# MLP up products of a two-model chain as seven quarter products

## The chip, the cores and the metric

The kernel runs on one core of a Trainium2 chip. The metric is the device time of one execution in microseconds (us). The engines are named as in the profile: PE is TensorE (PEld its weight loads), DVE is VectorE, ACT is ScalarE, POOL is GpSimd, SP is SyncE, which issues the weight transfers.

## What is computed

A first model of two layers (convolution and retention) is followed by a second of two layers: a state-space mixer with an MLP, and an attention over latents (MLA) with an MLP. All weights and activations are float32, 512 tokens of 1024 features; the second model puts 16 meta tokens ahead, so its first layer has 528. What matters here is the second model's frame and its MLPs:

```python
def rms_norm_2(x, gain):
    xf = x.astype(jnp.float32)
    y = xf * lax.rsqrt(jnp.mean(xf * xf, axis=-1, keepdims=True) + EPS)
    return (y * gain.astype(jnp.float32)).astype(x.dtype)

def sqrelu_mlp(h, w_up, w_down):            # w_up 1024 x 4096, w_down 4096 x 1024
    return jnp.square(jax.nn.relu(h @ w_up)) @ w_down

    for i in range(DEPTH):                  # DEPTH = 2
        hn = rms_norm_2(h, ln_mix[i])
        h = h + (ssd_mixer if i % 2 == 0 else mla_mixer)(hn, ...)
        h = h + sqrelu_mlp(rms_norm_2(h, ln_mlp[i]), mlp_w_up[i], mlp_w_down[i])
    return h[:, N_META:]
```

## The kernel before

Activations lie in SBUF with features on the 128 partitions and tokens along the free axis; the residual `xres` has 8 such feature tiles (k = 0 to 7) of 528 tokens. Products keep float32 accuracy by splitting each operand into a high and a low part (type fp32r): the high part is a cast on ACT, the low part a subtraction on DVE. A product is three matmuls, high x high, high x low and low x high, summed in PSUM: `mm3` (L226) with the weights stationary and the tokens moving, `mm3t` (L233) the other way round. PSUM has eight banks: `pb0` and `pb1` hold two each, `side0` to `side3` one each (`BANK[0]` to `BANK[7]`).

Weights come through `Stream`: a plan of tiles in the order of use, two buffers deep. `next(key)` hands out one tile and emits the next one: its transfers on SP's queue into `wraw`, four casts of 512 columns on ACT (L65, `whi`) and four low parts on DVE (L66, `wlo`). An order of instructions per engine is settled by a scheduler from the program's order and dependencies; each engine then runs its own list strictly in order.

The places that are touched:

- *State-space output passes* (`out_pass`, L746). The mixer's 16 result tiles `mix` (split pairs in a ring of nine buffers, `mixh`/`mixl`) are multiplied by the output weights in three passes of 8, 6 and 2 tiles. The last pass adds the last 2 tiles to all 8 feature tiles k and, tile by tile, adds into `xres` (L756, DVE), prepares the operand of the MLP (`prep`: gain and high part on ACT L218, low part on DVE L219) and sums the squares (`sq_acc`: squares on ACT L263, running sum on POOL L264). Then `rstd2` turns the sums into 1/rms: one matmul with ones (L269), a square root on ACT, a reciprocal on DVE (L274).
- *First MLP* (528 tokens as two halves of 264). Four blocks f; in each, four up steps (q; one weight tile of 1024 x 256) and four down steps (1024 x 256 each). An up step makes two feature tiles of 128 hidden columns: `dense2` with 8 feature tiles x 3 matmuls x 2 halves each; relu on ACT (L948), then on DVE a multiplication by R2, the square of 1/rms (L950), one by the relu (L951), and the split into the ring (L254 ACT, L255 DVE). The eight results of a block are then multiplied by the down tiles and added into `xres` (L963).
- *MLA setup* (`mla_setup`) stands in the second block of the first MLP.
- *MLA output passes and second MLP* (512 tokens). Two output passes of four result tiles each, the second with `prep` and `sq_acc`; then the same four blocks: up steps with 512 columns per matmul, down steps with tokens stationary (`mm3t`, 256 columns) into `rt`, token-major, added on DVE (L1310); the transposes of `xres` into `rt` stand after the first block's up steps.

## Time and profile before

| | us |
|---|---|
| runs | 2557.51, 2559.8, 2561.83 (median 2559.8) |
| profiled execution, its own time | 2556.87 |
| its span | 2555.1 |
| PE busy in it | 2500.3 |
| DVE busy | 1480.3 |
| ACT busy | 1001.2 |
| POOL busy | 182.6 |

The span is the time from the first to the last instruction in the profile; the execution's own time has 1.8 us around it. A row of the timeline has the start and the recorded length of one instruction or of several in a row (x2); recorded lengths of neighbours on one engine can overlap, so a cadence is read from starts. The view of waits counts idle time of an engine, put down to the instruction whose end released it. "Granted clock" (PEclk) is TensorE's clock as a share of its higher level.

### The profile page before, as it was taken

The page shows a single profiled execution, that of the slowest core. Times are in us where ns is not written, and L with a number is a line of the kernel's source. Part 1 is how long each engine was busy: PE and PEld are TensorE (multiplying, and loading weights), DVE is VectorE, ACT ScalarE, POOL GpSimd, SP SyncE. Part 2 cuts the span into 40 slices and gives each one's busy share as a digit, 9 for nine tenths or more (in the row PEclk, how much of TensorE's full clock was granted, in tenths as well). Part 3 has the DMA queues.
Part 4 walks back from the last instruction along what each step waited for, and adds up shares of the span by engine and source line. Part 5 has one row for each costly group of instructions (what it writes and reads, how often), then busy time and mean ns, then how long its engine had stood idle before and what let it go on. Part 6 is the DMA issues. An engine that isn't in the chain of part 4 may idle for free.

```text
span 2555.1 us, 40242 instructions
## 1 busy us (share of the span) xinstructions
PE 2500.3 (98%) x16657; PEld 2209.6 (86%) x16657; DVE 1480.3 (58%) x2893; ACT 1001.2 (39%) x2164; POOL 182.6 (7%) x208
## 2 busy tenths in 40 slices
PE   8989999999999999999999999999999999999999
PEld 7878888888888888899999999999997667799898
DVE  6733455474435555888848875434455765644443
ACT  4322333343223334555535543322344764423322
POOL 1000000010000001122112220000011000100000
PEclk9999999999999999999999999999999999999999
DMA  4443222223332222333333322323222111232322
GB/s 142 91 99 108 83 67 83 83 71 94 99 107 66 83 86 61 89 101 96 99 91 93 88 90 87 99 83 99 84 69 72 60 54 50 83 92 90 99 93 73
DMA packets 213383, 220.88 MB, mean 86 GB/s; under 512 B 8796, under 2 KB 203469, under 8 KB 213200
## 3 DMA queue, kind: packets, MB, share of 16 engines
q1 hardware_dynamic: 208512, 207.50, 26.6%
q0 software_dynamic: 4208, 10.68, 2.4%
q8 instruction: 130, 2.13, 0.3%
q14 instruction: 53, 0.43, 0.1%
q10 hardware_dynamic: 480, 0.13, 0.0%
HBM read 215.46 MB, written 2.83 MB: 85 GB/s over the span
## 4 chain that ended last, share of the span: by engine, by line
PE 86%; DVE 5%; ACT 3%; issue 3%; DMA 2%; POOL 1%; POOLq 0%; ACTq 0%; DVEq 0%
PE pb L226 53%; PE main L226 10%; PE main L233 8%; PE pb L233 4%; PE side L1221 1%; PE side L1234 1%; DMA ea<-ssd_a_log 1%; DVE wlo L66 1%; PE side L822 1%; PE main L1227 1%; PE side L831 1%; POOL sums L264 1%; PE side L560 1%; PE side L578 1%; PE side L580 1%
## 5 line engine op out<-in xcount | busy, mean ns | idle before, releaser
L65 ACT CAST whi<-wraw 128x512 fp32r<-128x512 f32 (+2 forms) x721 | 408.4, 622 | 886.2 <-PE pb L226 558.3
L66 DVE TENSOR_TENSOR wlo<-wraw,whi 128x512 fp32r<-128x512 f32 (+2 forms) x721 | 483.1, 711 | 209.6 <-ACT whi L65 208.5
L226 PE MATMUL pb<-xh_n,wlo 128*128 128x264 f32 (+3 forms) x1264 | 352.9, 325 | 0.0
L226 PE MATMUL pb<-xh_n,whi 128*128 128x264 f32 (+3 forms) x1264 | 348.5, 324 | 2.8 <-ACT xh_n L218 2.2
L226 PE MATMUL pb<-xl_n,whi 128*128 128x264 f32 (+3 forms) x1264 | 348.0, 324 | 0.0
L226 PEld LDWEIGHTS pb<-xh_n,whi 128*128 128x128 f32 (+1 forms) x1264 | 213.4, 188 | 23.0 <-ACT xh_n L218 2.5
L226 PEld LDWEIGHTS pb<-xh_n,wlo 128*128 128x128 f32 (+1 forms) x1264 | 214.6, 188 | 19.4 <-issue 1.4
L226 PEld LDWEIGHTS pb<-xl_n,whi 128*128 128x128 f32 (+1 forms) x1264 | 213.4, 188 | 17.7
L226 PE MATMUL pb<-xh_l,whi 128*128 128x512 f32 (+1 forms) x480 | 184.3, 384 | 12.1 <-ACT whi L65 11.0
L226 PE MATMUL pb<-xl_l,whi 128*128 128x512 f32 (+1 forms) x480 | 184.6, 385 | 0.8 <-DVE xl_l L219 0.8
L226 PE MATMUL pb<-xh_l,wlo 128*128 128x512 f32 (+1 forms) x480 | 184.0, 383 | 0.0
L233 PE MATMUL main<-whi,mh_w 128*128 128x256 f32 x512 | 144.3, 282 | 0.1
L233 PE MATMUL main<-whi,ml_w 128*128 128x256 f32 x512 | 143.5, 281 | 0.0
L233 PE MATMUL main<-wlo,mh_w 128*128 128x256 f32 x512 | 143.5, 281 | 0.0
L226 PEld LDWEIGHTS pb<-xh_l,whi 128*128 128x128 f32 x480 | 91.1, 190 | 31.3 <-ACT whi L65 11.8
L226 PEld LDWEIGHTS pb<-xl_l,whi 128*128 128x128 f32 x480 | 91.3, 190 | 18.4 <-DVE xl_l L219 1.2
L226 PEld LDWEIGHTS pb<-xh_l,wlo 128*128 128x128 f32 x480 | 91.2, 190 | 17.6 <-DVE wlo L66 0.2
L226 PE MATMUL pb<-xh_m,whi 128*128 128x264 f32 x512 | 104.5, 285 | 0.1
L226 PE MATMUL pb<-xl_m,whi 128*128 128x264 f32 x512 | 104.5, 285 | 0.0
L226 PE MATMUL pb<-xh_m,wlo 128*128 128x264 f32 x512 | 104.4, 285 | 0.0
L226 PE MATMUL pb<-ml_u,whi 128*128 128x264 f32 x512 | 104.0, 284 | 0.0
L226 PE MATMUL pb<-mh_u,whi 128*128 128x264 f32 x512 | 103.7, 284 | 0.0
(545 smaller groups left out, 5557.8 us busy)
## 6 DMA issues: line engine op xcount, KB each, us to landing
wraw<-w_in SPq DMA_DIRECT2D x64, 1024.0 KB, 6.0
wraw<-mlp_w_up SPq DMA_DIRECT2D x32, 1024.0 KB, 5.6
wraw<-mlp_w_down SPq DMA_DIRECT2D x32, 1024.0 KB, 5.1
wraw<-w_out SPq DMA_DIRECT2D x16, 1024.0 KB, 5.1
wraw<-ssd_w_in SPq DMA_DIRECT2D x16, 1024.0 KB, 5.3
wraw<-ssd_w_in SPq DMA_DIRECT2D x16, 512.0 KB
ab<-acsD POOLq DMA_DIRECT2D x32, 256.0 KB, 3.8
wraw<-ssd_w_out SPq DMA_DIRECT2D x5, 1024.0 KB
```

Source lines behind the costliest of these rows:

```text
L65: nc.scalar.copy(hv[s], rv[s])
L66: eng.tensor_tensor(lv[s], rv[s], hv[s].bitcast(F32), ALU.subtract)
L226: nc.tensor.matmul(ps, w[wq][:, k, wsl], x(xq, k, cs), start=(k == 0 and wq + xq == 0), stop=(k == nk - 1 and wq == 1))
L233: nc.tensor.matmul(ps, x(xq, k, ts_), w[wq][:, k, csl], start=(k == 0 and wq + xq == 0), stop=(k == nk - 1 and xq == 1))
L264: nc.gpsimd.tensor_tensor(dst, dst, v, ALU.add)
L560: nc.tensor.matmul(ch(A, c), ch(kT, c), ch(qT, c), start=True, stop=True)
L578: nc.tensor.matmul(ch(op, c), ch(pm, c), v[:, c, P * n : P * n + P], start=True, stop=(c == 0))
L580: nc.tensor.matmul(ch(op, c), ch(qT, c), ch(st, c - 1), start=False, stop=True)
L822: nc.tensor.matmul(o, xd[:W, h], M[:W, h, :W], start=True, stop=(c == 0))
L831: nc.tensor.matmul(st[:, :256], Bt[:W], xw[:W].rearrange("p h e -> p (h e)"), start=True, stop=True)
L1221: nc.tensor.matmul(sp_, Qh[:, h, q0 : q0 + M], Kh[:, h, :L], start=True, stop=False)
L1227: nc.tensor.transpose(pst[:, c, :M], p[:M, P * c : P * c + P], ident[:M, :M])
```

## The change

*Quarter products.* The 1024 x 256 weight tile is seen as a 2 x 2 of quarters (inner dimension in two halves of 512, hidden columns in two halves of 128), the operand as a 2 x 2 (inner halves, token halves). Seven products of quarters and sums of quarters give the four result quarters, with products numbered 1 to 7 (`m`): weights 11, 12, S4, 22, S1, S2, S3 against operands 11, 21, 22, T4, T1, T2, T3. Each is 4 inner tiles x 3 matmuls of half the tokens, into the next of the eight PSUM banks (`ringpos`). Product 1 is copied to SBUF by ACT (`su`), which empties its bank; seven DVE additions make the results. `Stream.seven` makes the weight sums: S1 to S3 in a scratch `wsr` with one buffer, S4 in place of the quarter 21 of the raw tile, each split by itself (`wsh`, `wsl`, three buffers each), and one cast and one low part over all 2048 columns. `Seven.prep` makes the operand sums T1 to T4, by pairs of feature tiles (k, k + 4), with scratch from the ring of nine. Relu and square are both on ACT now, and R2 is applied after the down products: in the first MLP by a second DVE instruction, in the second by one that takes R2 as a column per token.

*Output passes.* The state-space passes are now: 8 result tiles to all k; 6 to k = 0, 4, 1, 5 (weight tiles j = 0, 1 of two column stretches each); the last 2 to the same four; all 8 to k = 2, 6, 3, 7. Of these the last two, with `prep` by pairs, stand in the first MLP's scope. The second MLA pass goes by the same pairs.

*Later squares.* `sq_acc` moves from the output passes into the first two up steps, four tiles in each, and `rstd2` (in the second MLP `rstd` and four transposes for the column form of R2) behind the third.

The diff, cut to its core:

```diff
+    def seven(self, i, raw, hi, lo):
+        sr = self.spool.tile([P, 3, 512], F32, tag="wsr", name=f"wsr{i}", bufs=1)
...
+        def sums(n):
+            h, l = (self.spool.tile([P, 512], F32R, tag=f"ws{q}", name=f"ws{q}{i}{n}", bufs=3) for q in "hl")
+            nc.scalar.copy(h, sr[:, n])
+            V.tensor_tensor(l, sr[:, n], h.bitcast(F32), ALU.subtract)
+            return [t.rearrange("p (k c) -> p k c", k=4) for t in (h, l)]
...
+        V.tensor_tensor(s1, w["S4"], w["22"], ALU.add)
+        V.tensor_tensor(s3, w["11"], w["S4"], ALU.subtract)
+        V.tensor_tensor(s2, s1, w["11"], ALU.subtract)
+        V.tensor_tensor(w["S4"], w["12"], s2, ALU.subtract)
+        S1, S3 = sums(0), sums(1)
+        nc.scalar.copy(hi, raw)
+        V.tensor_tensor(lo, raw, hi.bitcast(F32), ALU.subtract)
+        S2 = sums(2)
...
+        def prep(self, k, g):
...
+            g_ = scratch("mixh", f"xg{j}")
+            nc.scalar.activation(g_, xres[:, k + 4 * j, hl], AF.Identity, scale=g)
+            a0, a1 = g_[:, :hw], g_[:, hw:]
+            if j == 0:
+                t = scratch("mixl", "xs")
+                V.tensor_tensor(t[:, :hw], a1, a0, ALU.subtract)
+                part(H[:, h0], L[:, h0], a0)
+                part(H[:, h1], L[:, h1], t[:, :hw])
+                self.raw[k] = g_, t
+                return
+            b, t = self.raw[k]
+            t2, t3, t4 = t[:, :hw], t[:, hw:], b[:, :hw]
+            V.tensor_tensor(t3, a1, b[:, hw:], ALU.subtract)
+            part(H[:, hl], L[:, hl], g_)
+            V.tensor_tensor(t2, a1, t2, ALU.subtract)
+            V.tensor_tensor(t4, a0, t2, ALU.subtract)
...
+    def product7(w, X, tmp, nm, order):
...
+        for n in order:
+            a, b = m[n]
+            ps = BANK[ringpos[0]][:, : X.hw]
+            ringpos[0] = (ringpos[0] + 1) % 8
+            for k in range(4):
+                for wq, xq in ((0, 0), (0, 1), (1, 0)):
+                    nc.tensor.matmul(ps, w[wq][a][:, k], X(xq, b, k), start=(k == 0 and wq + xq == 0),
+                                     stop=(k == 3 and wq == 1))
+            B[n] = ps
+            if n == 1:
+                B[1] = tmp("U", f"s{nm}", 4)
+                nc.scalar.copy(B[1], ps)
...
+    def up7(w, X, pool, cs, nm, first=False, bufs=3):
...
+        for n, i, p1, p2 in product7(w, X, tmp, nm, (1, 5, 2, 3, 7, 6, 4) if first else (5, 7, 6, 1, 3, 4, 2)):
+            o = r[n][:, X.hw * i : X.hw * i + X.hw]
+            V.tensor_tensor(o, p1, p2, ALU.add)
+        for n in range(2):
+            nc.scalar.activation(r[n], r[n], AF.Relu)
+            nc.scalar.activation(r[n], r[n], AF.Square)
+            m = mix_tile(f"{nm}{n}")
+            split(m, r[n], cs)
...
-                for n in range(2):
-                    nm = f"{f}{q}{n}"
-                    ps = dense2(w, n, X, 8)
-                    r = tmp(f"r{nm}")
-                    nc.scalar.activation(halves(r), ps, AF.Relu)
-                    t = mp.tile([P, T2], F32, tag="t", name=f"t{nm}", bufs=3)
-                    V.tensor_tensor(t, r, R2, ALU.mult)
-                    V.tensor_tensor(t, t, r, ALU.mult)
-                    m = mix_tile(f"u{nm}")
-                    split(m, t, slice(0, T2))
-                    mix.append(m)
+                mix += up7(w, X, mp, slice(0, T2), f"u{f}{q}", f + q == 0)
+                if f == 0 and q < 2:
+                    for k in range(4 * q, 4 * q + 4):
+                        sq_acc(tmp, sums, k, xres[:, k], f"ssq{k}")
+                if f == 0 and q == 2:
+                    rstd2(Rx, sums, D, BANK[4:6])
+                    V.tensor_tensor(R2, Rx, Rx, ALU.mult)
...
-                    xk = halves(xres[:, k])
-                    V.tensor_tensor(xk, ps, xk, ALU.add)
+                    t = tmp(f"d{f}{k}")
+                    V.tensor_tensor(halves(t), ps, halves(R2), ALU.mult)
+                    V.tensor_tensor(xres[:, k], t, xres[:, k], ALU.add)
...
-                    V.tensor_tensor(rt[:, b, ds_], ps, rt[:, b, ds_], ALU.add)
+                    V.scalar_tensor_tensor(rt[:, b, ds_], ps, R2[:, b : b + 1], rt[:, b, ds_], ALU.mult, ALU.add)
```

How it moves instructions is shown at three places. In the names the number after `wsh`, `whi` or `wraw` is the weight tile's (for `wsh` and `wsl` a last digit 0, 1, 2 stands for S1, S3, S2); the number behind the last underscore tells buffers apart.

PE, between two products of an up step in the first MLP. Before, where one tile of 128 hidden columns ends and the next begins (each row is two matmuls, one per half of the tokens):

```order
L226 MATMUL pb0_77<-xh1_m0_13269,whi131_15362 128x264 x2
L226 MATMUL pb0_77<-xl1_m0_13271,whi131_15362 128x264 x2
L226 MATMUL pb0_77<-xh1_m0_13269,wlo131_15363 128x264 x2
L226 MATMUL pb1_78<-xh0_m0_13268,whi132_15488 128x264 x2
L226 MATMUL pb1_78<-xl0_m0_13270,whi132_15488 128x264 x2
L226 MATMUL pb1_78<-xh0_m0_13268,wlo132_15489 128x264 x2
```

Now, in the second up step of the first block (tile 115), where product 1 ends and product 5, that of S1, begins:

```order
L326 MATMUL side2_72<-xh0_m0_13119,wlo115_13500 128x264
L326 MATMUL side2_72<-xh0_m0_13119,whi115_13499 128x264
L326 MATMUL side2_72<-xl0_m0_13121,whi115_13499 128x264
L326 MATMUL pb1_78<-xh0_m0_13119,wsh1150_13508 128x264
L326 MATMUL pb1_78<-xl0_m0_13121,wsh1150_13508 128x264
L326 MATMUL pb1_78<-xh0_m0_13119,wsl1150_13509 128x264
```

A bank now takes 12 matmuls of one half instead of 48 of both. In this step 12 matmuls of S3, 12 of S2 and 11 of product 1 stand ahead of those of S1, which in the program's order are not ahead of it.

DVE, in a later block of the first MLP, the third of four up steps. Before (`wraw`, `whi`, `wlo`: weight tile; `t`, `r`: result before the split):

```order
L950 TENSOR_TENSOR t210_15550<-r210_15548,R2_13446 128x528
L951 TENSOR_TENSOR t210_15550<-t210_15550,r210_15548 128x528
L255 TENSOR_TENSOR ml_u210_15554<-t210_15550,mh_u210_15553 128x528
L66 TENSOR_TENSOR wlo133_15615<-wraw133_15616,whi133_15614 128x512
L950 TENSOR_TENSOR t211_15607<-r211_15605,R2_13446 128x528
L66 TENSOR_TENSOR wlo133_15615<-wraw133_15616,whi133_15614 128x512
L951 TENSOR_TENSOR t211_15607<-t211_15607,r211_15605 128x528
L66 TENSOR_TENSOR wlo133_15615<-wraw133_15616,whi133_15614 128x512 x2
L255 TENSOR_TENSOR ml_u211_15611<-t211_15607,mh_u211_15610 128x528
L950 TENSOR_TENSOR t220_15676<-r220_15674,R2_13446 128x528
L951 TENSOR_TENSOR t220_15676<-t220_15676,r220_15674 128x528
L255 TENSOR_TENSOR ml_u220_15680<-t220_15676,mh_u220_15679 128x528
```

Now (`uu`, `vu`: partial sums; `ru`: results; L90 to L93 the weight sums):

```order
L90 TENSOR_TENSOR wsr132_15657<-wraw132_15655 128x512
L337 TENSOR_TENSOR uu20_15596<-side2_72,su20_15594 128x264
L91 TENSOR_TENSOR wsr132_15657<-wraw132_15655 128x512
L340 TENSOR_TENSOR vu20_15598<-uu20_15596,side0_70 128x264
L92 TENSOR_TENSOR wsr132_15657<-wsr132_15657,wraw132_15655 128x512
L359 TENSOR_TENSOR ru201_15545<-side1_71,vu20_15598 128x264
L346 TENSOR_TENSOR uu20_15596<-uu20_15596,side1_71 128x264
L359 TENSOR_TENSOR ru200_15544<-pb0_77,vu20_15598 128x264
L359 TENSOR_TENSOR ru200_15544<-pb1_78,su20_15594 128x264
L93 TENSOR_TENSOR wraw132_15655<-wraw132_15655,wsr132_15657 128x4x128
L359 TENSOR_TENSOR ru201_15545<-pb0_77,uu20_15596 128x264
L96 TENSOR_TENSOR wlo132_15654<-wraw132_15655,whi132_15653 128x2048
```

The seven additions of the step's products stand among the sums and low parts for the next weight tile, whose 2048-wide low part (L96) comes ahead of the split of the step's first result.

ACT, in the first block of the first MLP. Before, the second step's results beside the casts of the next weight tiles:

```order
L254 CAST mh_u001_13571<-t001_13568 128x528
L948 ACTIVATE r010_13635<-pb1_78 128x528
L254 CAST mh_u010_13640<-t010_13637 128x528
L65 CAST whi117_13701<-wraw117_13703 128x512
L948 ACTIVATE r011_13692<-pb0_77 128x528
L65 CAST whi117_13701<-wraw117_13703 128x512 x3
```

Now, from just behind the cast of S1 of the third tile (`wsh1160`) and the first relu of the first step (`ru000`):

```order
L411 ACTIVATE ssq1_13632<-xres_93 128x528
L363 ACTIVATE ru000_13522<-ru000_13522 128x528
L84 CAST wsh1161_13654<-wsr116_13645 128x512
L402 CAST mh_u000_13621<-ru000_13522 128x528
L362 ACTIVATE ru001_13523<-ru001_13523 128x528
L411 ACTIVATE ssq2_13635<-xres_93 128x528
L363 ACTIVATE ru001_13523<-ru001_13523 128x528
L411 ACTIVATE ssq3_13638<-xres_93 128x528
L402 CAST mh_u001_13627<-ru001_13523 128x528
L95 CAST whi116_13641<-wraw116_13643 128x2048
L84 CAST wsh1162_13660<-wsr116_13645 128x512
L332 COPY su01_13714<-side2_72 128x264
```

The squares for the norm (L411), relu and square of the first step's results (L362, L363) and the casts for the third tile stand ahead of `su01`, the copy of the second step's product 1.

## Rows read from the trace of the kernel before

**Rows 1.** The profile's page, span and busy time per engine.
```profile
span 2555.1 us, 40242 instructions
PE 2500.3 (98%) x16657; PEld 2209.6 (86%) x16657; DVE 1480.3 (58%) x2893; ACT 1001.2 (39%) x2164; POOL 182.6 (7%) x208
```

**Rows 2.** Waits of PE: line, waited for, us in total, times, longest.
```profile
PE side L269 <- POOL sums L264: 5.0, 4, 2.5
PE side L269 <- POOL asums L264: 1.2, 1, 1.2
PE pb L226 <- DVE xres L756: 0.9, 1, 0.9
```

**Rows 3.** First MLP by stretch: length, PE, PEld, DVE, ACT, POOL, PEclk, DMA share, GB/s.
```profile
1526.00:1574.00 48.00, 48.00 (x394) 48.00 (x394) 30.66 (x47) 18.27 (x32) 0.00 (x0) 1.00 0.33 102
```

**Rows 4.** Timeline of PE in the MLPs: start us, us, line, operation, tiles, shape.
```profile
1540.01 0.41 PE L226 MATMUL pb<-xh_m,wlo 128*128 128x264 f32 x2
...
1556.16 0.41 PE L226 MATMUL pb<-xh_m,wlo 128*128 128x264 f32 x2
...
2211.67 0.39 PE L226 MATMUL main<-xh_m,whi 128*128 128x512 f32 x1
...
2224.88 0.39 PE L226 MATMUL main<-xh_m,whi 128*128 128x512 f32 x1
...
2249.80 0.28 PE L233 MATMUL main<-whi,mh_w 128*128 128x256 f32 x1
...
2257.96 0.29 PE L233 MATMUL main<-whi,mh_w 128*128 128x256 f32 x1
```

**Rows 5.** Timeline of DVE in an up step; in brackets idle time and releaser.
```profile
1546.05 0.69 DVE L66 TENSOR_TENSOR wlo<-wraw,whi 128x512 fp32r<-128x512 f32 x1 [2.82 <-ACT whi L65]
1546.66 0.70 DVE L950 TENSOR_TENSOR t<-r,R 128x528 f32<-128x528 f32 x1
1547.28 0.68 DVE L66 TENSOR_TENSOR wlo<-wraw,whi 128x512 fp32r<-128x512 f32 x1
...
1552.18 0.71 DVE L950 TENSOR_TENSOR t<-r,R 128x528 f32<-128x528 f32 x1 [1.77 <-ACT r L948]
1552.92 0.71 DVE L951 TENSOR_TENSOR t<-t,r 128x528 f32<-128x528 f32 x1
```

**Rows 6.** Groups by line: busy us, mean ns of one, idle before, releasers.
```profile
L1310 DVE TENSOR_TENSOR rt<-main,rt 128x256 f32<-128x256 f32 x64 | 27.0, 423 | 108.1 <-PE main L233 108.1
...
L808 DVE TENSOR_TENSOR M<-M,cb 128x512 f32<-128x512 f32 x32 | 24.9, 778 | 0.0
...
L254 ACT CAST mh_u<-t 128x528 fp32r<-128x528 f32 x32 | 20.3, 635 | 34.9 <-DVE t L951 34.9
```

**Rows 7.** Timeline around the first MLP's start: casts of 2048, two reciprocals.
```profile
1496.24 1.92 ACT L65 CAST whi<-wraw 128x2048 fp32r<-128x2048 f32 x1 [7.13 <-issue]
...
1498.19 2.29 DVE L66 TENSOR_TENSOR wlo<-wraw,whi 128x2048 fp32r<-128x2048 f32 x1 [1.04 <-ACT whi L65]
...
1526.08 3.45 DVE L274 RECIPROCAL Rx<-Rx 128x264 f32<-128x264 f32 x2
```

**Rows 8.** Line 264: ns min/median/max, first and last start; DVE's timeline beside them.
```profile
L264 POOL TENSOR_TENSOR sums<-sums,ssq x7: 1622/1675/1847, 1511.5 to 1522.2; 128x528 f32<-128x528 f32 x7
L264 POOL TENSOR_TENSOR sums<-sums,msq x7: 1318/1484/1539, 1864.8 to 1899.8; 128x528 f32<-128x528 f32 x7
...
1509.72 0.77 DVE L219 SCALAR_TENSOR_TENSOR xl_m<-xres,vec,xh_m 128x528 fp32r<-128x528 f32 x1 [0.19 <-ACT xh_m L218]
...
1522.55 1.80 DVE L219 SCALAR_TENSOR_TENSOR xl_m<-xres,vec,xh_m 128x528 fp32r<-128x528 f32 x1
```

**Rows 9.** The same columns at the start and in the last output pass.
```profile
0.00:10.00 10.00, 4.12 (x17) 3.24 (x17) 3.30 (x14) 2.59 (x4) 0.21 (x4) 1.00 0.70 216
10.00:20.00 10.00, 6.03 (x32) 5.36 (x32) 6.74 (x15) 6.36 (x15) 3.01 (x4) 0.83 0.92 301
1515.00:1526.00 11.00, 8.35 (x63) 7.84 (x63) 11.00 (x12) 7.57 (x14) 8.39 (x6) 1.00 0.00 0
```

More of the change, by code (lines that the diff above doesn't have):

```diff
@@ L163, in build @@
         for q in range(2):
-            ws.add(("mo", i, q), [(0, mw_out[512 * i : 512 * i + 512, 512 * q : 512 * q + 512])], 4, 512)
+            src = mw_out[512 * i : 512 * i + 512]
+            ws.add(("mo", i, q), [(256 * n, src[:, 512 * n + 256 * q : 512 * n + 256 * q + 256]) for n in range(2)], 4, 512)
     plan_mlp(1)
@@ L219, in prep, with __init__, __call__, part @@
         V.scalar_tensor_tensor(X(1, k, cs), src, g, X(0, k, cs).bitcast(F32), ALU.mult, ALU.subtract)
+    class Seven:
+        def __init__(self, name, pool, hs):
+            self.x = Operand(name)
+            self.name, self.raw, self.hs = name, [None] * 4, hs
+            self.hw = hs[0].stop - hs[0].start
+            self.t = [pool.tile([P, 4, 3, self.hw], F32R, name=f"xt{q}_{name}") for q in "hl"]
+        def __call__(self, q, n, k):
+            if n in ("11", "T1", "21", "22"):
+                return self.x.t[q][n[0] == "2"][:, k, self.hs[n in ("T1", "22")]]
+            return self.t[q][:, k, int(n[1]) - 2]
+        def prep(self, k, g):
+            j, k = k // 4, k % 4
+            h0, h1 = self.hs
+            hl = slice(h0.start, h1.stop)
+            hw = self.hw
+            H, L = (self.x.t[q][j][:, k] for q in range(2))
+            def part(hi, lo, src):
+                nc.scalar.copy(hi, src)
+                V.tensor_tensor(lo, src, hi.bitcast(F32), ALU.subtract)
+            def scratch(tag, n):
+                return ring.tile([P, T2], F32, tag=tag, name=f"{n}{self.name}{k}", bufs=NRING)[:, : 2 * hw]
+            g_ = scratch("mixh", f"xg{j}")
[7 more added lines that the diff above has]
+                self.raw[k] = g_, t
+                return
+            b, t = self.raw[k]
[4 more added lines that the diff above has]
+            V.tensor_tensor(t4, a0, t2, ALU.subtract)
+            th, tl = (self.t[q][:, k] for q in range(2))
+            part(th[:, :2], tl[:, :2], t.rearrange("p (n c) -> p n c", n=2))
+            part(th[:, 2], tl[:, 2], t4)
@@ new lines, in build, with step @@
+    ringpos = [0]
+    def product7(w, X, tmp, nm, order):
+        m = {1: ("11", "11"), 2: ("12", "21"), 3: ("S4", "22"), 4: ("22", "T4"), 5: ("S1", "T1"), 6: ("S2", "T2"),
+             7: ("S3", "T3")}
+        B, steps = {}, set()
+        def step(n, *needs):
+            ready = n not in steps and all(i in B or i in steps for i in needs)
+            if ready:
+                steps.add(n)
+            return ready
+        for n in order:
[10 more added lines that the diff above has]
+                nc.scalar.copy(B[1], ps)
+            if step("11", 1, 2):
+                yield 0, 0, B[2], B[1]
+            if step("u", 1, 6):
+                u = tmp("U", f"u{nm}", 4)
+                V.tensor_tensor(u, B[6], B[1], ALU.add)
+            if step("v", "u", 5):
+                v = tmp("U", f"v{nm}", 4)
+                V.tensor_tensor(v, u, B[5], ALU.add)
+            if step("12", "v", 3):
+                yield 0, 1, B[3], v
+            if step("22", "v", 7):
+                yield 1, 1, B[7], v
+            if step("t", "u", 7):
+                V.tensor_tensor(u, u, B[7], ALU.add)
+            if step("21", "t", 4):
+                yield 1, 0, B[4], u
@@ L781, in build @@
             if g == 4:
-                out_pass(0, mix)
+                out_pass(0, mix, range(4))
                 mix = []
```

130 lines of the change are left out of this document (73 added, 57 removed).

## Prediction

> **What bounds the kernel now.** The page comes first: TensorE is busy 2500.3 of the span's 2555.1 us, 98% [rows 1]. Only work taken from TensorE, or a gap of its own closed, can shorten this kernel; anything added to another engine costs what it makes TensorE wait. The view of TensorE's waits shows the gaps beside the MLPs: 2.5 us for GpSimd's running sum of squares and 0.9 us for a residual add ahead of the first MLP, 1.2 us for the same running sum ahead of the second [rows 2]. Inside the MLPs there is none: busy 48.00 of 48.00 us in a stretch of the first [rows 3], and in the second the starts below are evenly spaced. So a stretch there lasts as long as its matmuls follow one another, which is read from starts in the timeline [rows 4]: 132 matmuls of 264 columns from 1540.01 to 1556.16, 0.1224 us each; 57 of 512 from 2211.67 to 2224.88, 0.2318; 69 of 256 from 2249.80 to 2257.96, 0.1183.
>
> **The quarter products.** An up step (one weight tile of 256 columns, 16 per MLP) now issues 7 x 4 x 3 = 84 matmuls of half the tokens. In the first MLP it was 2 x 8 x 3 x 2 = 96 of 264, so 12 x 0.1224 = 1.47 us less, times 16: **-23.5**. In the second it was 48 of 512, 11.13 us, and becomes 84 of 256, 9.94 at the third cadence (weights and tokens change sides against that row; I take it as it stands): 1.19 x 16 = **-19.0**. The three gaps of [rows 2] go too, since the sums of squares are now needed only by the down products, some 40 us later: **-4.6**. Best possible: -47.
>
> **What VectorE gets for it.** Back to back, a 512-wide instruction takes 0.61 us of the engine and a 528-wide one 0.62 (starts 1546.05, 1546.66, 1547.28), about 0.09 less than the recorded length; an instruction that needs the one before starts 0.74 after it (1552.18, 1552.92) [rows 5]. A 256-wide one that reads PSUM is recorded with 0.423, so 0.34, and 264 columns 0.35 [rows 6]; 2048 columns take VectorE 2.29 and ScalarE 1.92 [rows 7]. A step of the first MLP now needs four sums of quarters and three low parts, 7 x 0.61 = 4.3; one low part of 2048, 2.2; seven adds of the products, 7 x 0.35 = 2.4; two low parts of the result, 1.2: **10.1 us**, and with five dependent starts at 0.12 more 10.7, against TensorE's 84 x 0.1224 = 10.3. Before it was four low parts and three instructions for each of two results, 6.2. In the second MLP 10.0 stands against 9.9. The sums read runs of 128 elements with a stride, which the trace of before does not have: bounds are the recorded 0.69 of the plain 128x512 form [rows 5] and 0.78 of one with a broadcast operand [rows 6]; I take the plain one, as both operands are plain there; the other end adds 4 x 0.09 = 0.4 a step. So in a steady step VectorE is level with TensorE. What saves a block is that the first weight tile and half of the second are prepared during the down products ahead (47 us with little on VectorE): over four up steps it has 4 x 10.1 - 6.5 - 2.6 + 2.4 (the first down tile) = 33.7 of TensorE's 41. ScalarE has 1.83 + 3 x 0.53 + 6 x 0.54 + 0.35 = 7.0 a step [rows 6, 7]. Hence no price for steady blocks beyond 0.3 us each, for the places where order beats average: **+1**.
>
> **The first block of the first MLP.** Eight of nine ring buffers hold the operands of the last output pass, so the second scratch of the first pair is free only when the last tile (48 x 0.1224 = 5.9 us) has read its first operand. From there, some 1.4 us on (six matmuls and a ScalarE pass), VectorE has 25 instructions of 264 and 9 of 528 to make the operands, and 2.8 for the second weight tile: 8.8 + 5.6 + 2.8 = 17.2, done after 18.6. TensorE has 5.9 + 10.3 = 16.2 of work, and wants the last operand 16 matmuls (2.0 us) before its end: **+4**. Then the order shown for ScalarE decides. Its cast for the third tile's S1 waits for the second tile's S1 product, which stands behind 35 other matmuls of that step, 47 x 0.1224 = 5.8 us in. From there 3 casts of 512, 9 passes of 528, one of 2048 and the copy lie in line, 1.6 + 4.9 + 1.8 + 0.4 = 8.7 us [rows 6, 7]; TensorE, 25 matmuls (3.1 us) on, wants the bank that this copy empties: 5.6 late, and 1.2 more for the low part that follows it: **+7**. Two reciprocals, 3.45 us together [rows 7], now stand on VectorE in the middle of this block, ahead of results that are not yet due: **+1**. The second block repeats the bank wait in small, with the attention's set-up on VectorE too; from half of the first's: **+3**.
>
> **Squares beside VectorE.** GpSimd's seven adds move from the output pass, where TensorE had to wait for them, into the first two up steps. In the output pass the same adds took a median 1.675 us there against 1.484 in the down products, and one form of VectorE's with two operands in SBUF was recorded with 0.77 before they began and with 1.80 among them [rows 8]. I take half of that 1.03 for each of four instructions: **+2** in the first MLP; in the second it is in the next term. [...]
>
> **The first block of the second MLP.** The ring has free buffers here, so pairs are prepared as they come. In the last output pass and the first step (22.2 + 9.9 = 32.1 us) VectorE has 8 adds, 4 pairs of 3.6, the second weight tile's low parts 2.3 and two tiles of 6.5: 34.5, so 2.4 late; the same wait on ScalarE's order as above, in part, and one reciprocal, about as long as the two above: **+7**.
>
> **At no cost:** the output passes have 384 matmuls as before, and their loads, now two or four transfers of narrower rows on SP's queue, are asked for a tile ahead, under 11.7 us of products. The second multiply after each down product (0.62) lies under 5.9 us of matmuls per tile; without that cover it would be 32 x 0.62 = 20 us.
>
> **Sum:** -23.5 - 19.0 - 4.6 + 1 + 4 + 7 + 1 + 3 + 2 + 7 = **-22.1**. The profiled execution took 2556.87, so 2534.8; the median of the runs lies 2.9 above it: **2538**.
>
> **Rivals.** *The waits are hidden after all* (TensorE's order leaves slack, VectorE's pairs overlap): of the 25 us of new waits at most 10 stay, -37 to -42, 2518 to 2523. For it: gaps cost nothing where a bank is free. Against it: ScalarE is served strictly in the order shown. Chance 0.18. *VectorE becomes the bound in every step*, the other side. Each of 32 steps then lasts as long as its queue: with 12.0 us (strided sums at their upper bound, every dependent start, the semaphores of 17 instructions) it is 32 x 12.0 = 384 against 16 x 11.75 + 16 x 11.13 = 366 before, +18 less the old gaps 4.6, plus 6 for the first blocks: 2579. It decides from 11.4 us a step, 13% over my 10.1. For it: 10.1 and 10.3 are level already. Against it: 33.7 in 41 over a block. Chance 0.07 slower, and 0.07 that it takes back just the gain. [...] Chance 0.03.
>
> **How the numbers follow.** Forecast 0.65, 2526 to 2550; hidden 0.18; the rest as above. The range reaches from the hidden case to new waits 1.7 times as long as summed (25 x 1.7 = 42.5, so -4.6): 2519 to 2556. Within 0.2% (5 us, about what a measurement of this kernel can tell from no change) 0.07, slower 0.07, faster 0.86.
>
> **What would show it.** In the new profile: 84 matmuls in each up step, of 264 columns in the first MLP and 256 in the second; VectorE busy near 90% or more in up steps, under half in down steps; waits of TensorE gathered in the two first blocks, on the copy of product 1 and on low parts; later blocks within 1 us of 41.1 and 39.8 for four steps. Wrong would be waits in every block of over 3 us, steady steps over 10.8, or a granted clock below 1.

## The result, and the profile after

The changed kernel took 2540.6 us (median of 4 runs, 2538.6 to 2540.9) against 2560.8 before: ratio 0.9922, 95% interval 0.9906 to 0.9938. A second comparison of the same kernel (*The change again*, below) gave 2538.5 and 0.9914 (0.9899 to 0.9929). Forecast were 2538 and a range of 2519 to 2556: right in sign and size. The profiled execution (2538.6) has a span of 2536.8, 18.3 us under that of before.

The page of the new profile, to be read beside [rows 1]:

```profile
span 2536.8 us, 41634 instructions
...
PE 2467.7 (97%) x17045; PEld 2206.4 (87%) x17045; DVE 1644.6 (65%) x3204; ACT 1101.8 (43%) x2302; POOL 184.6 (7%) x208
```

TensorE has 32.6 us less work, VectorE 164 more. Of the 32.6, 14 came back as idle time. The view of TensorE's waits (columns as in [rows 2]) says where it waited for what is new:

```profile
PE side L417 <- POOL sums L412: 5.2, 4, 2.0
PE side L326 <- DVE xl_m L280: 4.5, 3, 2.3
...
PE side L326 <- ACT xh_m L279: 2.6, 2, 1.7
PE side L326 <- ACT su L332: 2.4, 1, 2.4
...
PE side L326 <- DVE wlo L96: 1.3, 1, 1.3
...
PE side L417 <- DVE uu L337: 0.8, 1, 0.8
```

The gaps of [rows 2] for the sums are not gone: the line has 5.2 us where it had 5.0, now with one of 2.0 in the first block and one of 1.8 behind the first MLP. Only the 1.2 ahead of the second MLP has no line any more. Busy time by stretch (columns as in [rows 3]) shows which stretches lost. The rows are the four up steps of a block: the first (with the norm) and the third of the first MLP, then the first and the second of the second MLP. The third row ends at transposes that stand ahead of the last 12 matmuls of its block; with these the block lasts until 2229.08, 48.56 us.

```profile
1520.43:1578.02 57.59, 49.36 (x343) 46.34 (x342) 52.50 (x81) 36.19 (x63) 12.56 (x7) 0.91 0.17 56
1714.64:1756.00 41.36, 41.36 (x338) 41.20 (x337) 34.63 (x59) 24.92 (x39) 0.00 (x0) 1.00 0.31 102
2180.52:2227.64 47.12, 41.35 (x337) 40.00 (x335) 46.44 (x71) 33.72 (x56) 7.65 (x6) 1.00 0.21 68
2277.48:2317.29 39.81, 39.81 (x339) 39.81 (x337) 32.66 (x58) 23.55 (x38) 0.00 (x0) 1.00 0.32 104
```

The third and the second block are all TensorE, 41.36 and 39.81 us for 336 matmuls, 0.1231 and 0.1185 each: as summed. The two first blocks have idle time, VectorE busy 52.50 of 57.59 and 46.44 of 47.12, and in the first MLP a granted clock of 0.91. The longest waits there, that for the norm behind the first MLP, and those of the second MLP's first block, in TensorE's timeline:

```profile
1547.49 0.39 PE L326 MATMUL side<-xh_m,whi 128*128 128x264 f32 x1 [2.37 <-ACT su L332]
...
1549.30 0.59 PE L326 MATMUL side<-xh_m,wlo 128*128 128x264 f32 x1 [1.30 <-DVE wlo L96]
...
1565.73 0.71 PE L417 MATMUL side<-sums,ones 128*128 128x264 f32 x2 [2.00 <-POOL sums L412]
...
1896.89 1.16 PE L417 MATMUL side<-sums,ones 128*128 128x264 f32 x4 [1.81 <-POOL sums L412]
...
2183.65 0.38 PE L326 MATMUL side<-xh_m,whi 128*128 128x256 f32 x1 [1.67 <-ACT xh_m L279]
...
2188.19 0.39 PE L326 MATMUL side<-xl_m,wsh 128*128 128x256 f32 x1 [1.78 <-DVE xl_m L280]
...
2194.56 0.38 PE L326 MATMUL side<-xl_m,whi 128*128 128x256 f32 x1 [2.32 <-DVE xl_m L280]
```

Between the same points of both traces (forecast: the prediction's terms by stretch; the first block's is -5.9 for its matmuls, -2.5 for the old gap, and 4 + 7 + 1 + 2):

| stretch | before | after | difference | forecast |
|---|---|---|---|---|
| start to the last norm of the state-space part | 1477.35 | 1479.89 | +2.5 | 0 |
| output passes | 40.80 | 40.54 | -0.3 | -0.9 |
| first MLP, first four up steps, norm | 50.74 | 57.59 | +6.9 | +5.6 |
| rest of the first MLP | 328.44 | 312.98 | -15.5 | -13.9 |
| from there to the norm behind it | 4.01 | 5.89 | +1.9 | 0 |
| attention and its output passes | 283.62 | 283.63 | 0.0 | 0 |
| second MLP, first block | 96.11 | 96.96 | +0.9 | +1.0 |
| rest | 274.03 | 259.32 | -14.7 | -14.0 |
| sum | 2555.1 | 2536.8 | -18.3 | -22.2 |

### The profile page after: what moved, and what is told of

Its sections match the earlier page's. It is cut to its first block, busy times and chain, and to the rows that moved or that the text cites. A ratio compares the mean times of both kernels' runs of the same rounds, so it can differ in the third digit from the quotient of the medians.

```text
span 2536.8 us, 41634 instructions
## 1 busy us (share of the span) xinstructions
PE 2467.7 (97%) x17045; PEld 2206.4 (87%) x17045; DVE 1644.6 (65%) x3204; ACT 1101.8 (43%) x2302; POOL 184.6 (7%) x208
## 5 line engine op out<-in xcount | busy, mean ns | idle before, releaser
L68 ACT CAST whi<-wraw 128x512 fp32r<-128x512 f32 (+1 forms) x595 | 336.4, 620 | 621.8 <-PE pb L374 430.5
L69 DVE TENSOR_TENSOR wlo<-wraw,whi 128x512 fp32r<-128x512 f32 (+1 forms) x595 | 396.8, 706 | 135.6 <-ACT whi L68 134.5
L374 PE MATMUL pb<-xh_l,whi 128*128 128x512 f32 (+1 forms) x480 | 184.9, 386 | 13.6 <-ACT whi L68 13.1
L374 PEld LDWEIGHTS pb<-xh_l,whi 128*128 128x128 f32 x480 | 91.6, 191 | 32.7 <-ACT whi L68 13.9
L95 ACT CAST whi<-wraw 128x2048 fp32r<-128x2048 f32 x32 | 61.1, 1908 | 119.9 <-issue 53.9
L84 ACT CAST wsh<-wsr 128x512 fp32r<-128x512 f32 x96 | 58.9, 616 | 111.9 <-DVE wsr L90 51.7
L374 PE MATMUL pb<-mh_u,wlo 128*128 128x264 f32 x512 | 103.6, 284 | 0.0
```

Source lines behind the costliest of these rows:

```text
L68: nc.scalar.copy(hv[s], rv[s])
L69: eng.tensor_tensor(lv[s], rv[s], hv[s].bitcast(F32), ALU.subtract)
L84: nc.scalar.copy(h, sr[:, n])
L95: nc.scalar.copy(hi, raw)
L374: nc.tensor.matmul(ps, w[wq][:, k, wsl], x(xq, k, cs), start=(k == 0 and wq + xq == 0), stop=(k == nk - 1 and wq == 1))
```

## The experiments

Theory A at the outset: what the change loses, it loses in the two first blocks, to the order in which ScalarE and VectorE do small things there, the squares above all. Its rival B: VectorE has too much work there, in whatever order.

**One part alone.** Quarter products in the second MLP only.

```diff
-ws.add(("up", i, f, q), [...], 8, 256, seven=True)
+ws.add(("up", i, f, q), [...], 8, 256, seven=i == 1)
```

> Quarter products in the second MLP alone (with its later squares and pairwise output pass); the first MLP and the state-space passes as before. Theory A (the two parts add up, and what the trace of the change shows per stretch is the change's own): from the end of the attention to the end of the kernel the new trace is 13.8 us shorter, so 13.8 us less than before, 2547; second MLP's first four up steps with about 6 us of waits, later blocks 39.8 for four steps. Theory B (the first MLP's part gives nothing, or is part of the second's gain): 18 to 20 us less, 2541 to 2543.

Measured 2546.7 against 2557.4, ratio 0.9955 (0.9940 to 0.9969), 10.7 less; from the norm behind the first MLP to the end the trace is 12.1 shorter. That is on A's side, 2 to 3 short of its number: the second MLP brings 11 to 14 of the 20, the first the rest.

**Late squares with direct products.** Squares and norm as in the change, in the kernel before.

```diff
-                    V.tensor_tensor(t, r, R2, ALU.mult)
-                    V.tensor_tensor(t, t, r, ALU.mult)
+                    V.tensor_tensor(t, r, r, ALU.mult)
...
+                if f == 0 and q < 2:
+                    for k in range(4 * q, 4 * q + 4):
+                        sq_acc(tmp, sums, k, xres[:, k], f"ssq{k}")
```

> The kernel before with direct products, but the squares for both norms in the first two up steps and their factor applied after the down products. Theory A (the three old gaps go, VectorE has room in direct steps, and the second multiply behind the last down product stands on the path): -4.6 for the gaps, +1.9 at the norm behind the first MLP, in all 2 to 3 us less than before. Theory B (the squares cost as much wherever they stand, since GpSimd holds VectorE beside them and TensorE waits for VectorE): no gain, 0 to +2.

Measured 2555.0, ratio 0.9990 (0.9980 to 0.9999): 2.4 less, as A had it. The first four up steps fall from 50.74 to 47.86 without a wait, and the way to the norm behind the MLP grows from 4.0 to 5.3. With VectorE busy 30.72 of 47.86 us there, the late squares make TensorE wait for nothing in these steps. That points to the fuller VectorE of the change (52.50 of 57.59) as a condition of what they cost there.

**Squares on VectorE.** What GpSimd does beside VectorE is seen in the changed kernel's timeline. First two of GpSimd's additions, then VectorE's instructions (start, length) in the same stretch:

```profile
1540.00 1.80 POOL L412 TENSOR_TENSOR sums<-sums,ssq 128x528 f32<-128x528 f32 x1 [60.15 <-ACT ssq L411]
...
1548.13 2.27 POOL L412 TENSOR_TENSOR sums<-sums,ssq 128x528 f32<-128x528 f32 x1 [2.25 <-ACT ssq L411]
```
```profile
1539.94 0.68 DVE L92 TENSOR_TENSOR wsr<-wsr,wraw 128x512 f32<-128x512 f32 x1
1540.54 1.82 DVE L85 TENSOR_TENSOR wsl<-wsr,wsh 128x512 fp32r<-128x512 f32 x1
1542.28 0.69 DVE L403 TENSOR_TENSOR ml_u<-ru,mh_u 128x528 fp32r<-128x528 f32 x1
1542.89 1.81 DVE L93 TENSOR_TENSOR wraw<-wraw,wsr 128x512 f32<-128x512 f32 x1
1544.63 1.79 DVE L85 TENSOR_TENSOR wsl<-wsr,wsh 128x512 fp32r<-128x512 f32 x1
...
1549.16 1.79 DVE L85 TENSOR_TENSOR wsl<-wsr,wsh 128x512 fp32r<-128x512 f32 x1
```

Forms of 512 and 528 columns take 0.68 to 0.70, and 1.79 to 1.82 where they start while one of GpSimd's additions runs; six do so in this block (four of them shown), 6 x 1.1 = 6.6 us. So the additions were given to VectorE:

```diff
-            nc.gpsimd.tensor_tensor(dst, dst, v, ALU.add)
+            eng.tensor_tensor(dst, dst, v, ALU.add)   # V in the up steps
```

> The change, with the running sums of squares of the first up steps added on VectorE in place of GpSimd (seven additions of 528 and seven of 512). Theory A (GpSimd's additions hold VectorE: six instructions of 1.8 in place of 0.69 us cost 6.6 us there, the additions on VectorE itself only 4.3): the first four up steps of the first MLP, 57.6 with the norm, become 54 to 55.5, no VectorE instruction of 512 columns there is recorded with 1.8, and the whole is 2 to 4 us under the change. Theory B (VectorE is short of time by the amount of its work alone): 4.3 us more work in that block, so 1 to 4 us slower than the change.

Measured 2534.2, ratio 0.9903 (0.9888 to 0.9918), 3 to 5 under the change by the ratios. The block is 54.22, and none of VectorE's instructions of 512 columns in it is recorded with 1.8 any more: A's numbers. But the gain of this block is the clock's. Its granted clock was 1.00, and against 336 matmuls at 0.1224 the block loses 13.1 us; the change's loses 16.5 in the first profile and 16.2 in the second (*The change again*), 3.9 and 3.3 of them at low clock (matmuls at 0.22 in place of 0.12), so 12.6 and 12.9 without it. What TensorE no longer waits at the copy and the low part (1.62 and 1.03, for 2.37 and 1.30) it waits more at the norm (3.5, for 2.8). The second MLP's first block, with a clock of 1.00 here and in the change's first profile, fell from 48.56 to 46.86, and the waits for operands shown above are gone from it (others, 4.2 in sum, came in their place). So VectorE's loss of 6.6 is seen on VectorE; that it costs TensorE time is shown for the second MLP, 1.7. Whether the shorter wait for the copy is what spared the low clock here is not shown.

**No squares.** Seven of eight feature tiles' squares left out of both norms.

```diff
-                if f == 0 and q < 2:
-                    for k in range(4 * q, 4 * q + 4):
+                if f == 0 and q < 1:
+                    for k in range(1):
```

> The change, but with seven of the eight squares and all running sums left out of both norms ahead of the MLPs (so these norms are of one feature tile). Theory A (the squares lengthen VectorE's instructions, stand in ScalarE's line ahead of the copy of product 1, and are late for the norm): the wait for the copy (2.4), for the low part (1.3), the low clock behind them (2.7) and the wait for the sums (2.0 and 0.8) go or halve, the first four up steps of the first MLP fall from 57.6 to 49 to 51, the second MLP's by 1 to 3, the whole 7 to 11 under the change. Theory B (the operands and the order of ScalarE's casts are the cause): only the waits for the sums go, 3 us under the change.

Measured 2526.2, ratio 0.9875 (0.9858 to 0.9891), 10 to 12 under the change, at A's upper end and above. The block is 50.04, that of the second MLP 44.95 instead of 48.56. Of the first block's 7.5, 3.9 is the low clock of the change's first profile. Its row and the two waits left behind the operands:

```profile
1520.23:1570.27 50.04, 45.51 (x342) 42.55 (x341) 46.57 (x83) 32.53 (x56) 0.00 (x0) 1.00 0.20 66
```
```profile
1544.43 0.39 PE L326 MATMUL side<-xh_m,whi 128*128 128x264 f32 x1 [0.30 <-ACT su L332]
...
1546.63 0.39 PE L326 MATMUL side<-xh_m,wlo 128*128 128x264 f32 x1 [1.69 <-DVE wlo L96]
```

The copy of product 1 is 0.30 late, not 2.37. The low part is 1.69 late, not half of 1.30 as A said: that wait is not the squares'.

**The change again.** The same kernel, for a second profile.

> The change itself, as the comparison for the two runs beside it and as a second profile of it. Theory A (the stretches of low granted clock in the first block come with gaps but not with every such gap: the run with squares on VectorE had the same waits for operands at 1531 us and no low clock there): the waits are the same within 0.3 us, the low stretches differ, and the four first up steps last 53 to 58. Theory B (they belong to the change's gaps): low clock in the same two places, 57.6 again.

A held: the waits for the copy, the low part, the sums and the partial sum are 2.33, 1.30, 1.97 and 0.80 (first profile 2.37, 1.30, 2.00, 0.80). The block is 57.36, so B's number came too. The granted clock (third column from the end) fell in other places, one of them the same. First profile, then second:

```profile
1530.00:1535.00 5.00, 4.41 (x20) 3.56 (x20) 4.31 (x10) 2.57 (x5) 0.00 (x0) 0.66 0.61 194
1550.00:1555.00 5.00, 5.00 (x24) 4.98 (x24) 4.79 (x10) 0.00 (x0) 0.40 (x1) 0.50 0.64 213
```
```profile
1530.00:1535.00 5.00, 3.96 (x27) 3.33 (x27) 4.31 (x10) 3.00 (x6) 0.00 (x0) 1.00 0.53 179
1550.00:1555.00 5.00, 4.87 (x34) 4.87 (x34) 4.35 (x11) 1.43 (x3) 0.00 (x0) 0.80 0.48 167
1565.00:1570.00 5.00, 4.92 (x26) 4.86 (x27) 5.00 (x10) 1.49 (x4) 0.00 (x0) 0.66 0.00 0
```

In both the clock falls behind the long wait for the copy: to 0.50 for the whole 5 us, and to 0.80; in the first also around 1531, behind the waits for operands, in the second also behind the wait for the sums. At 0.50 24 matmuls started in 5 us, 0.21 each. Nothing was varied between the two, so what decides whether the clock falls behind a gap stays open.

**VectorE's margin.** One sum of quarters computed four times.

```diff
-        V.tensor_tensor(s3, w["11"], w["S4"], ALU.subtract)
+        for _ in range(4):
+            V.tensor_tensor(s3, w["11"], w["S4"], ALU.subtract)
```

> The change, with one sum of weight quarters computed four times in place of once: three more VectorE instructions of 512 columns (3 x 0.61 = 1.83 us) in each of the 32 up steps, nothing else. Theory A (the weight tiles prepared during the down products cover four steps, 33.7 us of VectorE in 41, so 1.85 a step are free): blocks after the first of each MLP stay within 1.5 us of 41.4 and 39.8, the first blocks grow by 3 to 6 each, the whole by 5 to 15. Theory B (VectorE, level with TensorE in a step, is the bound from there on): every block grows by 4 x 1.5, the whole by 40 to 55.

Measured 2558.5, ratio 0.9995 (0.9985 to 1.0005): 20 more than the change, between the two numbers and nearer to A's. The first blocks grew by 3 and by 5 to 6.5, the second block of the first MLP by 5.1 (47.74 for 42.65); the rows are the third and fourth block of the first MLP and the second of the second:

```profile
1722.37:1765.74 43.37, 41.61 (x338) 41.13 (x337) 38.24 (x65) 24.57 (x38) 0.00 (x0) 1.00 0.30 97
1812.55:1857.43 44.88, 43.17 (x338) 42.69 (x337) 38.25 (x65) 24.48 (x38) 0.00 (x0) 0.96 0.29 95
2295.94:2335.69 39.75, 39.75 (x338) 39.75 (x337) 36.74 (x64) 23.88 (x38) 0.00 (x0) 1.00 0.33 108
```

39.75 in the second MLP: 1.83 us more a step cost nothing there, so B, which had every block grow by 6, is out for it. In the first MLP the later blocks cost 5.1, 2.0 and 3.5 more, in the last two with a wait of 1.55 for the last step's low part:

```profile
1755.61 0.39 PE L327 MATMUL side<-xh_m,wlo 128*128 128x264 f32 x1 [1.55 <-DVE wlo L97]
```

So A's 1.5 failed there: the margin of the first MLP is under 1.83 us a step, and VectorE is near to being its bound. That the second multiply, which fills its down products too, takes the margin is not shown.

**Four buffers.** Squares on VectorE, four buffers for split sums in the first MLP, and the last running sum behind it on VectorE.

```diff
-for q in "hl": ... name=f"ws{q}{i}{n}", bufs=3
+for q in "hl": ... name=f"ws{q}{i}{n}", bufs=self.wsb   # 4, second MLP 3
```

> Squares of the up steps added on VectorE as before, four buffers in place of three for the split weight sums of the first MLP, and the last running sum of squares behind the first MLP on VectorE. Theory A (ScalarE's cast of a sum waits for a buffer that a product of two tiles earlier holds, and holds the copy of product 1 back): the wait for the copy, 1.6 with squares on VectorE, falls under 0.6, the first four up steps of the first MLP from 54.2 to 51 to 53; the norm behind that MLP comes 1 us earlier; in all 2 to 4 under the run with squares on VectorE alone. Theory B (buffers are not what ScalarE waits for, VectorE's late sums are): only the 1 us at the norm.

Measured 2531.4, ratio 0.9886 (0.9871 to 0.9900), 3 under squares on VectorE alone by the medians, 4 by the ratios. But that is not A's doing: the waits at the norm in the block shrank (3.5 to 0.6) and the norm behind the MLP comes 1.1 us sooner, while the copy is 1.87 late (1.62 before). A fourth buffer does not take that wait away. Buffers are not out as a part of it: ScalarE's casts of sums still wait for products, 0.66 and 1.54 us here, and more buffers were not tried. ScalarE's timeline shows one of these waits, and what stands ahead of the copy without a gap:

```profile
1534.30 0.62 ACT L84 CAST wsh<-wsr 128x512 fp32r<-128x512 f32 x1 [1.54 <-PE side L326]
...
1539.99 0.63 ACT L411 ACTIVATE ssq<-xres 128x528 f32<-128x528 f32 x1
1540.52 0.62 ACT L402 CAST mh_u<-ru 128x528 fp32r<-128x528 f32 x1
1541.04 0.64 ACT L411 ACTIVATE ssq<-xres 128x528 f32<-128x528 f32 x1
1541.59 1.88 ACT L95 CAST whi<-wraw 128x2048 fp32r<-128x2048 f32 x1
1543.38 0.37 ACT L332 COPY su<-side 128x264 f32<-128x264 f32 x1
```

Two squares, a cast and the cast of 2048 columns. The last matmul of the product that is copied started at 1537.30, six us before.

**Squares spread, and casts of 512.** Two ways to take things out of that line, and both together. Spread: the squares of four feature tiles in the last output pass, two in the second and two in the third step (`SQ`: tiles 0, 4, 1, 5, 2, 6, 3, 7). Casts: `hi` and `lo` of an up tile in four pieces.

```diff
-                if f == 0 and q < 2:
-                    for k in range(4 * q, 4 * q + 4):
-                        sq_acc(tmp, sums, k, xres[:, k], f"ssq{k}", V)
+                if f == 0 and q in (1, 2):
+                    for k in range(2 * q + 2, 2 * q + 4):
+                        sq_acc(tmp, sums, k, xres[:, SQ[k]], f"ssq{k}", V)
...
-        nc.scalar.copy(hi, raw)
-        V.tensor_tensor(lo, raw, hi.bitcast(F32), ALU.subtract)
+        for c in range(0, 2048, 512):
+            d = slice(c, c + 512)
+            nc.scalar.copy(hi[:, d], raw[:, d])
+            V.tensor_tensor(lo[:, d], raw[:, d], hi[:, d].bitcast(F32), ALU.subtract)
```

> The kernel of the run before (squares added on VectorE, four buffers, last running sum on VectorE), with the first MLP's squares spread: those of feature tiles 0, 4, 1, 5 in the last output pass, where ScalarE and VectorE have idle time, the other four in the second and third up steps. Theory A (the squares stand ahead of the copy of product 1 in ScalarE's line): the wait for the copy, 1.87, falls under 0.6, the first four up steps of the first MLP from 53.2 to 50 to 51.5 (50.0 without squares), and the whole is 1.5 to 3 lower, 2528.5 to 2530. Theory B (VectorE's amount of work bounds the block, wherever the squares stand): the output pass or the operands take what the steps gain, no difference over 1.

> The kernel of the run before, with the cast and low part of 2048 columns of each up tile as four of 512 each. In ScalarE's order the copy of the second step's product 1 then stands 11 rows further ahead, before the squares and most casts. Theory A (the copy is late by its place in ScalarE's line, not by ScalarE's or VectorE's amount of work): the wait for the copy goes (under 0.3), the low part's wait behind it falls from 1.55 to under 1, the first four up steps fall from 53.2 to 51 to 52; later blocks, with 0.24 more of VectorE a step, stay at 41.3 and 39.8; the whole is 1 to 3 lower. Theory B (the amount of work): a wait for a low part or for a sum takes the place of that for the copy, the block stays at 53 or longer, the whole the same or 1 to 5 higher.

> Both edits of the two runs before together. Theory A: the first four up steps of the first MLP at 49 to 51, no wait over 1 us between the last operand and the norm, the whole 2.5 to 5 under the kernel with four buffers. Theory B: as that kernel, within 1.5 us.

Measured 2531.0, 2532.9 and 2531.2 (ratios 0.9888, 0.9897, 0.9892, each within 0.0017): none clear of the kernel with four buffers. The wait for the copy is gone in all three, as A said, and the time did not follow, as B said, because another wait took its place. With the squares spread, then with casts of 512, then with both:

```profile
1562.27 0.56 PE L326 MATMUL pb<-xth_m,wsh 128*128 128x264 f32 x1 [4.79 <-DVE uu L346]
```
```profile
1542.13 0.39 PE L328 MATMUL side<-xh_m,whi 128*128 128x264 f32 x1 [0.99 <-ACT whi L97]
...
1559.87 0.68 PE L419 MATMUL side<-sums,ones 128*128 128x264 f32 x2 [1.20 <-DVE sums L414]
```
```profile
1545.36 0.39 PE L328 MATMUL side<-xh_m,whi 128*128 128x264 f32 x1 [1.40 <-DVE uu L339]
...
1559.61 0.56 PE L328 MATMUL pb<-xth_m,wsh 128*128 128x264 f32 x1 [3.77 <-DVE uu L348]
```

The casts of 512 had a price of their own, 4 us in the second MLP's first block, where the clock fell to 0.93. The row is that block with both edits; with the squares spread alone it lasts 46.86:

```profile
2170.77:2221.76 50.99, 45.80 (x347) 43.41 (x346) 47.35 (x91) 34.03 (x64) 0.00 (x0) 0.93 0.21 69
```

So the casts were kept for the first MLP alone in the last kernel below.

**The norm after the fourth step.**

```diff
-                if f == 0 and q == 2:
+                if f == 0 and q == 3:
                     rstd2(Rx, sums, D, BANK[4:6])
...
+        step = 512 if self.wsb == 4 else 2048     # second run only: casts of 512 in the first MLP
```

> The run with the squares spread, with both norms (one matmul group with ones, square root, reciprocals, square) placed after the fourth up step in place of the third. Theory A (the two reciprocals, 3.6 us of VectorE in the middle of the block, stand ahead of the partial sums that empty TensorE's banks: the wait of 4.8 for a partial sum in the third step): that wait goes, the first four up steps of the first MLP fall from 54.0 to 47 to 50 with no wait over 1 us after the operands; the second MLP's, 46.9, to 44 to 46; the first down product's wait for the norm is under 1.5; the whole is 4 to 7 lower, 2524 to 2527. Theory B (VectorE owes the same work and TensorE waits for it somewhere): the wait comes back at the first down products, the whole within 2 of 2531.

> As the run beside it, with the cast and low part of 2048 columns as four of 512 in the first MLP alone (in the second the four cost 4 us: 50.9 against 46.9). Theory A: the wait for a low part (0.5) goes too; the first four up steps at 47 to 49, later blocks 41.2; the whole 0 to 1.5 under the run beside it. Theory B: 0 to 2 above it, VectorE's 0.24 a step more coming back as a wait.

Measured 2527.0 (ratio 0.9867, 0.9852 to 0.9882) and 2523.3 (0.9855, 0.9839 to 0.9872), 12 to 14 and 15 to 17 under the change. The 4.79 fell to 0.50, but not for the reason given: with the norm after the third step the reciprocals start at 1568.54, after that wait. The order of TensorE shows the reason. With the norm after the third step, its two matmuls (L417) need banks `side0` and `side1`, and the product that waits for `uu` stands ahead of them; without them there, two whole products for those banks stand first. Runs of matmuls, with their count:

```
norm after the third step              norm after the fourth
pb0_77 <- xh1, whi116  12              pb0_77 <- xh1, whi116  12
pb1_78 <- xth, wsh1171  5  (waits)     side1_71 <- xh1, whi117  12
pb0_77 <- xh0, wsh1170 12              side0_70 <- xh0, whi117  12
pb1_78 <- xth, wsh1171  5              pb1_78 <- xth, wsh1171  10
side0_70 <- sums, ones                 pb0_77 <- xh0, wsh1170  12
```

24 x 0.1224 = 2.9 us of work lie in the gap. In the last kernel the first blocks are these:

```profile
1519.14:1566.33 47.19, 44.74 (x343) 42.35 (x341) 45.66 (x94) 34.81 (x68) 0.00 (x0) 1.00 0.28 90
2165.29:2210.81 45.52, 41.21 (x339) 40.14 (x338) 44.60 (x83) 30.81 (x53) 0.00 (x0) 1.00 0.29 93
```

47.19 us for what took 57.59 (3.9 of the difference is the low clock's), at a clock of 1.00, and TensorE is idle for 2.5 us of it in place of 8.2. That does not put theory B, too much work for VectorE, out for the first block. VectorE's busy time in it fell from 52.50 to 45.66: half of the squares stand in the output pass, GpSimd no longer lengthens six instructions, and the reciprocals now stand behind the block's end at 1566.33:

```profile
1569.39 1.80 DVE L425 RECIPROCAL Rx<-Rx 128x264 f32<-128x264 f32 x1 [1.74 <-ACT Rx L424]
```

And 45.66 is still more than the 41.1 of TensorE's matmuls. That order counts is shown by the 24 matmuls above, with the reciprocals behind the wait; how much of the 10.4 us is order and how much is work taken out of the block was not measured apart.

## Why the prediction was right

- **The quarter products** (-23.5, -19.0): steady blocks of 41.36 and 39.81 instead of 46.98 and 44.47, so -5.6 and -4.7 a block where 5.9 and 4.75 were summed. "No price for steady blocks" held: 41.36 is 0.2 over 336 x 0.1224. So did its cover: VectorE has 34.63 us in four steady up steps, where 33.7 were summed.
- **The first block of the first MLP** (+4, +7, +1, +2). By starts in the first profile, against 336 matmuls at 0.1224: 4.2 lost up to the last operand, 1.2 behind it with the clock at 0.66, 4.2 around the copy and the low part, 2.7 at low clock behind them, 4.2 at the norm with its own matmuls (1.2). The operands' +4 is borne out, in the second profile too (4.2). The +7 for ScalarE's order was 4.2 of waits; that the 2.7 of low clock behind them fill it up is luck, as no term of the sum is for the clock. The place was right, and so was what stands in ScalarE's line: 9.3 us from the start of its first cast to the end of the copy (1538.17 to 1547.43), where 8.7 were summed. What failed is when the line starts:

```profile
1538.17 0.62 ACT L84 CAST wsh<-wsr 128x512 fp32r<-128x512 f32 x1 [1.78 <-DVE wsr L90]
```
```profile
1541.78 0.28 PE L326 MATMUL pb<-xh_m,wsl 128*128 128x264 f32 x1
```

The cast for the third tile's S1 waited for VectorE's sum, and not for the second tile's S1 product, whose last matmul (second row) starts 3.6 us later. So the copy was 2.4 late and not 5.6.
- **Squares beside VectorE** (+2) was mis-sized on VectorE: six instructions of 1.1, not four of 0.5: beside GpSimd's additions 0.69 becomes 1.80 in the trace. What it cost on the path of the first MLP is not shown, since the gain of squares on VectorE is the clock's there.
- **The old gaps** (-4.6): wrong in part. The 0.9 for the residual add is still there (0.91), and the sums are waited for again, 2.0, since ScalarE gave the squares late (GpSimd stood idle for them 2.11 and 0.76 us ahead of its last two additions). The step that failed: the sums are needed not only by the down products but, sooner, by the norm's own matmuls, which stand in TensorE's line behind the third up step.
- **At no cost** failed at one tile. Behind the first MLP the last tile's second multiply has no cover, and with a low part put between them and a GpSimd addition of 2.19 beside VectorE the norm comes 1.9 later (1.3 in the second profile, where that addition took 1.58).
- **The second block** (+3) was 1.2: 42.65 where steady blocks take 41.36, against 47.09 and 46.98 before. **The second MLP's first block** (+7) came within 0.2 as a whole, by luck: its operands were waited for 5.8 us (1.67, 1.78, 2.32) where 2.4 was summed, and for ScalarE's order, a part of the +7, there was no wait for the copy at all. The waits for operands are gone where GpSimd adds no squares (*Squares on VectorE*, *No squares*).
- **The signs.** The waits lie in the two first blocks and the later blocks are as said, but VectorE's share is 84 and 82% in steady up steps (near 90% was named; the prediction's own 33.7 of 41 is 82%) and 59% in the down steps ahead of the third block (under half was named), and a granted clock below 1, named as a sign of being wrong, did come (0.66 and 0.50 in stretches of 5 us). The row of those down steps:

```profile
1667.72:1714.64 46.92, 46.92 (x386) 46.74 (x385) 27.62 (x41) 13.40 (x22) 0.00 (x0) 1.00 0.28 91
```

- **The rival "VectorE becomes the bound in every step"** is out for the change: TensorE is busy 41.36 of 41.36 and 39.81 of 39.81 us in steady blocks. But the first MLP has under 1.83 us a step to spare (*VectorE's margin*). **"The waits are hidden after all"** is what the last kernel reaches by moving work: 2523.3, at the end of that case's 2518 to 2523. **The granted clock** fell, to which the prediction gave 0.03: to 0.66 and 0.50 in stretches of 5 us, some 40 matmuls at 0.22 in place of 0.12, so 4 us lost in the first profile. The change's steady blocks, whose products go round eight banks, stay at 1.00, and in the first block only stretches behind gaps fall, not each: behind the wait of 2.00 for the sums at 1565.73 the first profile has 1.00, the second 0.66.

In the profiled execution the sum is 3.9 short of the forecast: the +2.5 at the start and the +1.9 at the norm had no term, and the low clock stands against those waits of the second block that did not come. The median of the runs is nearer, 20.2 under that of before where 22 were forecast.

## What to carry to other kernels

When work is taken from the busiest engine, price the first pass through the new scheme by itself: here steady state had its cover (TensorE busy 41.36 of 41.36 us), the first block less (49.36 of 57.59), and there the amount and the order of small instructions on the helping engines decided. A wait that is removed shows the next one only in a new profile; two edits (squares, casts) gave nothing until the third (the norm a step later) was made. An addition moved to an idle engine can be dearer than on the busy one: here six instructions of VectorE grew by 1.1 us each beside GpSimd's additions, where seven additions of 0.62 on VectorE itself do the same work. And before a gain is put down to an edit, compare the granted clock of the two profiles: that of the first block was the clock's (1.00 against 0.91).

## What was not expected

- The first weights were waited for longer in the profile of the changed kernel, in work that the change does not touch. Before, then after:

```profile
12.94 0.39 PE L226 MATMUL pb<-xh_l,whi 128*128 128x256 f32 x1 [3.20 <-ACT whi L65]
```
```profile
13.87 0.58 PE L374 MATMUL pb<-xh_l,whi 128*128 128x256 f32 x1 [4.56 <-ACT whi L68]
```

At the end of the state-space part that and smaller waits had become 2.5 us; the runs with quarter products stood there 1.2 to 5.3 us behind, that with direct products and late squares 0.6. The wait for the first weights itself does not go with quarter products: it is 1.92 with the sum computed four times, 2.50 and 3.06 in the last two kernels, 4.95 in the change's second profile. Why is open: it was not tried.
- The clock's low stretches change place between two profiles of one kernel whose waits agree within 0.04 us: 0.66 and 1.00 from 1530 to 1535, 0.50 and 0.80 from 1550 to 1555.
